# Layer normalisation without affine terms: a ring of larger tiles, normalised in place, and a last store in two parts

## The chip, the cores and the metric

The kernel runs on one core of a Trainium2 chip, alone. The metric is the device time of one execution in microseconds (us), taken as the median of several. Three engines of the core compute here: VectorE (DVE in the profile), ScalarE (ACT) and GpSimd (POOL). SyncE (SP) only issues loads. The core's 16 DMA engines move data between the chip's main memory (HBM) and the on-chip buffer of 128 partitions (SBUF). SP and ACT each have one DMA queue, which runs over all 16 engines; a DMA is cut into packets, and each engine works through its own share of them.

## The reference

```
batch, seq, dim = 32, 512, 1024        # x is float32

def reference(x, eps):
    mean = np.mean(x, axis=-1, keepdims=True)
    var = np.var(x, axis=-1, keepdims=True)
    return ((x - mean) / np.sqrt(var + eps)).astype(np.float32)
```

There are 32 x 512 = 16,384 rows of 1,024 numbers, 4 KiB each: 64 MiB are read and 64 MiB are written. Each row is normalised by its own mean and variance.

## The kernel before, in words

The rows are laid out as a matrix of 16,384 x 1,024 (L23 to L25). A tile is 4 rows on each of 128 partitions (`K = 4`, L30), 512 rows or 2 MiB, so there are 32 tiles (L33). In a tile, partition p holds 4 rows that are neighbours in HBM; a partition's part of a load or store is thus one run of 16 KiB.

For every tile the loop (L43) does this:

- L46 and L47: SP issues the load into `xt`, one of six buffers (`xin`, L35).
- L51 to L57: for each of the 4 rows DVE runs two `bn_stats` over 512 columns each (L53) and one `bn_aggr` (L57) that joins them to a mean and a variance in `mv`.
- L59, L61, L65: DVE makes `negmean`, `vpe` (variance plus eps) and its reciprocal `ivar`, for the four rows at once.
- L68: ACT takes the square root of `ivar`, which gives `rstd`.
- L71: POOL multiplies `negmean` and `rstd` to `nmr`.
- L75: ACT makes four rows of `yt` from `xt`, as `rstd * x + nmr`, one instruction a row. `yt` is one of six other buffers (`yout`, L36).
- L84: ACT issues the store of `yt`.

Six buffers of 16 KiB a partition for `xt` and six for `yt` come to 192 KiB a partition. The framework sets the order of instructions on each engine itself from the dependencies, and it puts in the waits: a load into a buffer waits until ACT has read what was there, and L75 waits until the store of the earlier content of its `yt` has landed. The framework deals eight semaphores to the DMAs in turn (the trace has eight of them, with 128 landings each, 16 for a DMA). A DMA waits until the DMA that had its semaphore before has landed.

Of the kernel before, what the change touches and what calls it, by code (L numbers as in the profile page):

```python
# [1 line left out]

# [4 lines left out]


@with_exitstack  # L10
def kernel(
    ctx: ExitStack,
    tc: tile.TileContext,
    x: bass.AP,
    eps: bass.AP,
    out: bass.AP,
):
    nc = tc.nc
    P = nc.NUM_PARTITIONS

    eps_val = float(eps) if not isinstance(eps, bass.AP) else 1e-5

    x2 = x.flatten_outer_dims()  # L23
    o2 = out.flatten_outer_dims()
    N, D = x2.shape  # L25
    BN_MAX = nc.vector.BN_STATS_FMAX
    assert D % BN_MAX == 0
    NSUB = D // BN_MAX

    K = 4  # L30
    rows_per_tile = P * K
    assert N % rows_per_tile == 0
    ntiles = N // rows_per_tile  # L33

    xin = ctx.enter_context(tc.tile_pool(name="xin", bufs=6))  # L35
    yout = ctx.enter_context(tc.tile_pool(name="yout", bufs=6))  # L36
    st = ctx.enter_context(tc.tile_pool(name="st", bufs=4))

    fdt = mybir.dt.float32
    AF = mybir.ActivationFunctionType  # L40
    ALU = mybir.AluOpType

    for t in range(ntiles):  # L43
        rows = slice(t * rows_per_tile, (t + 1) * rows_per_tile)

        xt = xin.tile([P, K, D], fdt)  # L46
        nc.sync.dma_start(out=xt, in_=x2[rows].rearrange("(p k) d -> p k d", p=P))  # L47

        stats = st.tile([P, K, NSUB, 6], fdt)
        mv = st.tile([P, K, 2], fdt)  # L50
        for k in range(K):  # L51
            for s in range(NSUB):
                nc.vector.bn_stats(  # L53
                    out=stats[:, k, s, :],
                    in_=xt[:, k, s * BN_MAX : (s + 1) * BN_MAX],
                )
            nc.vector.bn_aggr(out=mv[:, k, :], in_=stats[:, k, :, :])  # L57
        negmean = st.tile([P, K], fdt)
        nc.vector.tensor_scalar_mul(out=negmean, in0=mv[:, :, 0], scalar1=-1.0)  # L59
        vpe = st.tile([P, K], fdt)  # L60
        nc.vector.tensor_scalar(  # L61
            out=vpe, in0=mv[:, :, 1], scalar1=eps_val, scalar2=None, op0=ALU.add
        )
        ivar = st.tile([P, K], fdt)
        nc.vector.reciprocal(out=ivar, in_=vpe)  # L65

        rstd = st.tile([P, K], fdt)
        nc.scalar.activation(out=rstd, in_=ivar, func=AF.Sqrt, bias=0.0, scale=1.0)  # L68

        nmr = st.tile([P, K], fdt)  # L70
        nc.gpsimd.tensor_mul(out=nmr, in0=negmean, in1=rstd)  # L71

        yt = yout.tile([P, K, D], fdt)
        for k in range(K):
            nc.scalar.activation(  # L75
                out=yt[:, k, :],
                in_=xt[:, k, :],
                func=AF.Identity,
                bias=nmr[:, k : k + 1],
                scale=rstd[:, k : k + 1],  # L80
            )

        dst = o2[rows].rearrange("(p k) d -> p k d", p=P)
        nc.scalar.dma_start(out=dst, in_=yt)  # L84


# [1 line left out]
_INS = ['x', 'eps']  # L88
_OUTS = [((32, 512, 1024), 'float32')]
#: Inputs that are plain numbers.  # L90
_NUMBERS = {'eps': 1e-05}


# [26 lines left out]
```

## Time and profile before

| what | value |
| --- | --- |
| median of 8 runs | 321.3 us (321.08 to 321.51) |
| the profiled execution, its own time | 321.35 us |
| its span, first to last profiled instruction | 319.3 us |
| DVE busy | 181.6 us, 57% of the span |
| ACT busy | 154.2 us, 48% |
| POOL busy | 6.6 us, 2% |
| moved by DMA | 134.27 MB, mean 421 GB/s |
| one `bn_stats` of 128 x 512 (L53), mean | 664 ns, 256 of them |
| one row on ACT (L75), mean | 1,227 ns, 128 of them |
| a load, issue to landing, median | 38.4 us |
| a store, issue to landing, median | 15.5 us |

The execution's own time is 2.05 us more than the span; what lies around the span isn't in the profile. The span is what the steps of the work can be read from. The DMA row of the profile gives the mean busy share of the 16 DMA engines: 1.00 says that all sixteen were busy, 0.06 that one of sixteen was. Packets of one engine can overlap by some nanoseconds, so that a share of 1.01 can be read. Beside the answers of the views, the trace holds a record of each DMA packet (start, duration, size and queue, but not the number of the engine), and single packets are quoted from there.

### The profile page before, as it was taken

Reading aid. Unit: us, or ns where it says so; the run is one execution under the profiler, and the core shown is the slowest. Engines: PE = TensorE matmul, PEld = TensorE weight load, DVE = VectorE, ACT = ScalarE, POOL = GpSimd, SP = SyncE. Lnnn points to the kernel's source line nnn. Section 1 sums busy time; section 2 is a strip of 40 time slices with the busy share of each in tenths; the row PEclk is TensorE's granted clock in tenths of the full one; section 3 lists DMA queues with packets and bytes.
Section 4 is the critical chain, followed back from the end, with each engine's and each line's share of the span. In section 5 each row is a group of like instructions: output and inputs, shape, how many; then the busy total and the mean of one; then the engine's idle time right before and its main releaser. Section 6 shows DMA issues by size and latency. Waiting matters only on the chain.

```text
span 319.3 us, 926 instructions
## 1 busy us (share of the span) xinstructions
DVE 181.6 (57%) x480; ACT 154.2 (48%) x161; POOL 6.6 (2%) x36
## 2 busy tenths in 40 slices
DVE  0999764457754477544676535765446744467610
ACT  1147491651907419074380833808347091470970
POOL 0000000000000000000000000000000000000000
DMA  7999999999999999999999999999999999999995
GB/s 298 427 394 426 435 435 431 431 429 429 428 431 434 433 431 427 429 429 433 435 435 431 428 429 429 429 431 435 433 433 426 426 431 435 433 433 413 419 427 220
DMA packets 9222, 134.27 MB, mean 421 GB/s; under 512 B 1024, under 2 KB 1024, under 8 KB 1024
## 3 DMA queue, kind: packets, MB, share of 16 engines
q1 hardware_dynamic: 4608, 67.11, 49.6%
q10 hardware_dynamic: 4608, 67.11, 49.2%
q14 instruction: 6, 0.05, 0.0%
HBM read 67.11 MB, written 67.11 MB: 420 GB/s over the span
## 4 chain that ended last, share of the span: by engine, by line
DMA 84%; ACT 4%; issue 4%; DVE 4%; SPq 1%; POOLq 0%; POOL 0%; ACTq 0%; DVEq 0%
DMA xt<-in_x_dram 84%; ACT yt L75 4%; DVE stats L53 3%; SPq L47 1%; DVE mv L57 0%; ACT rstd L68 0%; DVE ivar L65 0%; DVE negmean L59 0%; POOLq L115 0%; POOL nmr L71 0%; DVE vpe L61 0%; ACTq L84 0%; DVEq L65 0%; DVEq L59 0%; ACTq L75 0%
## 5 line engine op out<-in xcount | busy, mean ns | idle before, releaser
L53 DVE BATCH_NORM_STATS2 stats<-xt 128x6 f32<-128x512 f32 x256 | 159.4, 664 | 115.6 <-DMA xt<-in_x_dram 115.6
L75 ACT ACTIVATE yt<-xt,nmr,rstd 128x1024 f32<-128x1024 f32 x128 | 146.7, 1227 | 4.7 <-POOL nmr L71 4.5
L68 ACT ACTIVATE rstd<-ivar 128x4 f32<-128x4 f32 x32 | 6.5, 204 | 149.9 <-DVE ivar L65 149.3
L57 DVE BATCH_NORM_AGGREGATE mv<-stats 128x2 f32<-128x12 f32 x128 | 25.1, 196 | 1.1
L71 POOL TENSOR_TENSOR nmr<-negmean,rstd 128x4 f32<-128x4 f32 x32 | 6.3, 198 | 298.1 <-ACT rstd L68 298.1
L65 DVE RECIPROCAL ivar<-vpe 128x4 f32<-128x4 f32 x32 | 5.7, 178 | 3.0
L59 DVE TENSOR_SCALAR negmean<-mv 128x4 f32<-128x4 f32 x32 | 5.4, 170 | 3.1
L61 DVE TENSOR_SCALAR vpe<-mv 128x4 f32<-128x4 f32 x32 | 5.2, 162 | 0.0
L68 ACT ACT_TABLE_LOAD x1 | 1.3, 1283 | 0.7 <-PEq L101 0.7
L101 POOL MEMSET const-float32-0.0<- 128x1 f32 x1 | 0.1, 98 | 0.2 <-issue 0.2
L101 POOL MEMSET const-uint8-127<- 128x1 uint8 x1 | 0.1, 102 | 0.0
L101 POOL MEMSET const-bfloat16-1.0<- 128x1 bf16 x1 | 0.1, 101 | 0.0
L101 POOL MEMSET const-float32-1.0<- 128x1 f32 x1 | 0.1, 98 | 0.0
## 6 DMA issues: line engine op xcount, KB each, us to landing
xt<-in_x_dram SPq DMA_DIRECT2D x32, 2048.0 KB, 38.4
out_dram<-yt ACTq DMA_DIRECT2D x32, 2048.0 KB, 15.5
```

The costliest lines, as they stand in the source:

```text
L47: nc.sync.dma_start(out=xt, in_=x2[rows].rearrange("(p k) d -> p k d", p=P))
L53: nc.vector.bn_stats(out=stats[:, k, s, :], in_=xt[:, k, s * BN_MAX : (s + 1) * BN_MAX],)
L57: nc.vector.bn_aggr(out=mv[:, k, :], in_=stats[:, k, :, :])
L59: nc.vector.tensor_scalar_mul(out=negmean, in0=mv[:, :, 0], scalar1=-1.0)
L61: nc.vector.tensor_scalar(out=vpe, in0=mv[:, :, 1], scalar1=eps_val, scalar2=None, op0=ALU.add)
L65: nc.vector.reciprocal(out=ivar, in_=vpe)
L68: nc.scalar.activation(out=rstd, in_=ivar, func=AF.Sqrt, bias=0.0, scale=1.0)
L71: nc.gpsimd.tensor_mul(out=nmr, in0=negmean, in1=rstd)
L75: nc.scalar.activation(out=yt[:, k, :], in_=xt[:, k, :], func=AF.Identity, bias=nmr[:, k : k + 1], scale=rstd[:, k : k + 1],)
L101: nc = _bacc.Bacc("TRN2", target_bir_lowering=False, num_devices=1)
```

## The change

The new kernel has one ring of 48 rows a partition (192 KiB) in the place of the two pools. Its tiles are of 8 rows, 15 of them, then one of 6 and one of 2 (`TILES`): 32 KiB, 24 KiB and 8 KiB a partition. Six tiles of 8 rows fill the ring. ACT writes the normalised rows over the loaded ones, and the store reads the ring. So a load into a place of the ring waits for the store of what was there, six tiles before.

The arithmetic runs in groups of up to 4 rows, 33 in all. ACT takes the square root of the variance plus eps (the bias of the activation), DVE takes the reciprocal of it, and one `scalar_tensor_tensor` on DVE makes `nmr`. `negmean`, `vpe` and POOL's multiplication are gone. The instructions of each engine are in the order of the program text (`manual_schedule`). `STORE` is 16, more than a tile has, so each tile has one store, after its last group. The last store, that of the tile of 2 rows, is issued as two DMAs, one of partitions 0 to 119 and one of partitions 120 to 127.

```diff
+TILES = (8, 8, 8, 8, 8, 8, 8, 8, 8, 8, 8, 8, 8, 8, 8, 6, 2)
+RING = 48
+GROUP = 4
+STORE = 16
...
-    K = 4
-    rows_per_tile = P * K
-    ntiles = N // rows_per_tile
-
-    xin = ctx.enter_context(tc.tile_pool(name="xin", bufs=6))
-    yout = ctx.enter_context(tc.tile_pool(name="yout", bufs=6))
+    ring_pool = ctx.enter_context(tc.tile_pool(name="ring", bufs=1))
...
+    ring = ring_pool.tile([P, RING, D], fdt)
+    eps_t = const.tile([P, 1], fdt)
+    def load(t):
+        K, row, pos = plan[t]
+        rows = slice(row * P, (row + K) * P)
+        nc.sync.dma_start(
+            out=ring[:, pos : pos + K, :],
+            in_=x2[rows].rearrange("(p k) d -> p k d", p=P),
+        )
...
-        negmean = st.tile([P, K], fdt)
-        nc.vector.tensor_scalar_mul(out=negmean, in0=mv[:, :, 0], scalar1=-1.0)
-        vpe = st.tile([P, K], fdt)
-        nc.vector.tensor_scalar(
-            out=vpe, in0=mv[:, :, 1], scalar1=eps_val, scalar2=None, op0=ALU.add
+        std = st.tile([P, GROUP], fdt, name="std")
+        nc.scalar.activation(
+            out=std[:, :G], in_=mv[:, :G, 1], func=AF.Sqrt, bias=eps_t, scale=1.0
         )
-        ivar = st.tile([P, K], fdt)
-        nc.vector.reciprocal(out=ivar, in_=vpe)
-        rstd = st.tile([P, K], fdt)
-        nc.scalar.activation(out=rstd, in_=ivar, func=AF.Sqrt, bias=0.0, scale=1.0)
-        nmr = st.tile([P, K], fdt)
-        nc.gpsimd.tensor_mul(out=nmr, in0=negmean, in1=rstd)
+        rstd = st.tile([P, GROUP], fdt, name="rstd")
+        nc.vector.reciprocal(out=rstd[:, :G], in_=std[:, :G])
+        nmr = st.tile([P, GROUP], fdt, name="nmr")
+        nc.vector.scalar_tensor_tensor(
+            out=nmr[:, :G],
+            in0=mv[:, :G, 0],
+            scalar=-1.0,
+            in1=rstd[:, :G],
+            op0=ALU.mult,
+            op1=ALU.mult,
+        )
...
             nc.scalar.activation(
-                out=yt[:, k, :],
+                out=xt[:, k, :],
                 in_=xt[:, k, :],
...
+    def store(t, o, n):
+        K, row, pos = plan[t]
+        rows = slice(row * P, (row + K) * P)
         dst = o2[rows].rearrange("(p k) d -> p k d", p=P)
-        nc.scalar.dma_start(out=dst, in_=yt)
+        src = ring[:, pos + o : pos + o + n, :]
+
+        cuts = ((0, 120), (120, P)) if t == len(TILES) - 1 else ((0, P),)
+        for a, b in cuts:
+            nc.scalar.dma_start(out=dst[a:b, o : o + n, :], in_=src[a:b])
+    plan = []
+    row = pos = 0
+    for K in TILES:
+        if pos + K > RING:
+            pos = 0
+        plan.append((K, row, pos))
+        row += K
+        pos += K
+    with tc.manual_schedule():
+        nc.vector.memset(eps_t, eps_val)
+        for t, (K, row, pos) in enumerate(plan):
+            load(t)
+            sent = 0
+            for g in range(0, K, GROUP):
+                G = min(GROUP, K - g)
+                group(ring[:, pos + g : pos + g + G, :], G)
+                if g + G - sent >= STORE or g + G == K:
+                    store(t, sent, g + G - sent)
+                    sent = g + G
```

More of the change, by code (lines that the diff above doesn't have):

```diff
@@ L26 @@
     BN_MAX = nc.vector.BN_STATS_FMAX
-    assert D % BN_MAX == 0
     NSUB = D // BN_MAX
-    K = 4
-    rows_per_tile = P * K
-    assert N % rows_per_tile == 0
-    ntiles = N // rows_per_tile
-    xin = ctx.enter_context(tc.tile_pool(name="xin", bufs=6))
-    yout = ctx.enter_context(tc.tile_pool(name="yout", bufs=6))
+    assert sum(TILES) * P == N
+    ring_pool = ctx.enter_context(tc.tile_pool(name="ring", bufs=1))
     st = ctx.enter_context(tc.tile_pool(name="st", bufs=4))
+    const = ctx.enter_context(tc.tile_pool(name="const", bufs=1))
     fdt = mybir.dt.float32
@@ L41, with group @@
     ALU = mybir.AluOpType
[L43 to L51, printed above, removed]
+    ring = ring_pool.tile([P, RING, D], fdt)
[7 more added lines that the diff above has]
+        )
+    def group(xt, G):
+        stats = st.tile([P, GROUP, NSUB, 6], fdt, name="stats")
+        mv = st.tile([P, GROUP, 2], fdt, name="mv")
+        for k in range(G):
             for s in range(NSUB):
@@ L57 @@
             nc.vector.bn_aggr(out=mv[:, k, :], in_=stats[:, k, :, :])
-        negmean = st.tile([P, K], fdt)
-        nc.vector.tensor_scalar_mul(out=negmean, in0=mv[:, :, 0], scalar1=-1.0)
-        vpe = st.tile([P, K], fdt)
-        nc.vector.tensor_scalar(
-            out=vpe, in0=mv[:, :, 1], scalar1=eps_val, scalar2=None, op0=ALU.add
-        )
-        ivar = st.tile([P, K], fdt)
-        nc.vector.reciprocal(out=ivar, in_=vpe)
-        rstd = st.tile([P, K], fdt)
-        nc.scalar.activation(out=rstd, in_=ivar, func=AF.Sqrt, bias=0.0, scale=1.0)
-        nmr = st.tile([P, K], fdt)
-        nc.gpsimd.tensor_mul(out=nmr, in0=negmean, in1=rstd)
-        yt = yout.tile([P, K, D], fdt)
-        for k in range(K):
+        std = st.tile([P, GROUP], fdt, name="std")
+        nc.scalar.activation(
+            out=std[:, :G], in_=mv[:, :G, 1], func=AF.Sqrt, bias=eps_t, scale=1.0
+        )
+        rstd = st.tile([P, GROUP], fdt, name="rstd")
[9 more added lines that the diff above has]
+        )
+        for k in range(G):
             nc.scalar.activation(
-                out=yt[:, k, :],
+                out=xt[:, k, :],
                 in_=xt[:, k, :],
```

## The prediction

> **What bounds the kernel now.** I read the page first: the busy row, the DMA row by slices, the queues, the chain.
>
> ```profile
> span 319.3 us, 926 instructions
> ...
> DVE 181.6 (57%) x480; ACT 154.2 (48%) x161; POOL 6.6 (2%) x36
> ...
> DMA  7999999999999999999999999999999999999995
> ...
> q1 hardware_dynamic: 4608, 67.11, 49.6%
> q10 hardware_dynamic: 4608, 67.11, 49.2%
> ...
> DMA 84%; ACT 4%; issue 4%; DVE 4%; SPq 1%; POOLq 0%; POOL 0%; ACTq 0%; DVEq 0%
> ```
>
> No compute engine passes 57%. The DMA engines are full in all slices but the first and the last, loads and stores take half of them each, and 84% of the chain is loads. So only three things can shorten the span: fewer nanoseconds a byte, the start, and the tail. For those I asked for the busy time in chosen stretches (columns: length, DVE, ACT, POOL, clock, share of the 16 DMA engines, GB/s).
>
> ```profile
> 1.75:3.00 1.25, 0.00 (x0) 0.26 (x1) 0.00 (x0) 1.00 1.12 236
> ...
> 20.00:24.00 4.00, 4.00 (x10) 0.20 (x1) 0.20 (x1) 1.00 0.98 352
> 24.00:288.00 264.00, 155.04 (x412) 133.66 (x140) 5.56 (x28) 1.00 1.01 431
> ...
> 294.00:302.00 8.00, 4.01 (x12) 6.97 (x7) 0.20 (x1) 1.00 0.92 391
> 302.00:315.00 13.00, 2.17 (x8) 7.24 (x8) 0.20 (x1) 1.00 1.02 435
> 315.00:316.00 1.00, 0.00 (x0) 0.00 (x0) 0.00 (x0) 1.00 0.28 115
> 316.00:318.00 2.00, 0.00 (x0) 0.00 (x0) 0.00 (x0) 1.00 0.06 25
> ```
>
> For 264 us the rate is flat at 431 GB/s. From 294 to 302 the engines lack work for a moment (0.92 against 1.01). The last row matters most: 0.06 is 1/16, **one engine working alone for 2 us** after the others are done.
>
> The packet records say why. Fifteen engines end between 315.5 and 316.0, most near 315.6; one ends at 318.14, with four 16 KiB packets more to do. In the steady stretch (after 26 us) only six packets last over 660 ns, where the others take about 611; each follows an 8 KiB packet of queue 14, kind "instruction", that is code fetched for an engine, of 309 ns. Four of them chain to the late engine (29.5, 101.5, 180.2, 249.1 us; the next packet then takes 1,144 to 1,232 ns), so it loses 0.31 + 0.57, or 0.88 us, each time, 3.5 us in all. The two others (82.4 and 239.8 us; the next packet takes 849 and 856 ns) lie on another engine and cost 0.55 us each. Part of the late engine's lag doesn't show at the end, since the others starved at 294 to 302 and it didn't.
>
> **The change, part by part**, against the profiled execution: last packet 318.14, span 319.3 (1.16 later), own time 321.35 (2.05 more). The median, 321.3, is within 0.05 of that.
>
> *Larger packets.* Each engine moves 8 partitions of every tile: 288 records a queue and engine are 32 x 8 packets and 32 marks of 4 bytes that tell of completion. A 16 KiB packet starts 607 ns after the one before it, an 8 KiB one occupies 305 ns; 2 x 305 - 607 leaves about 3 ns a packet that don't scale. Before, an engine has 512 data packets; after, 2 x (15 x 8 + 8 + 8) = 272. That is 240 x 3 ns = 0.72 us less. Rounding of the records allows 1 to 5 ns (0.2 to 1.2 us), and nothing is gained if the hardware cuts 32 KiB in two. I take 0.72. Marks fall from 64 to 35 an engine at 5 ns: 0.15 us. Together **0.87 us** on all engines.
>
> *The last store in two.* 120 of 128 partitions are 15 engines' shares of 8; the natural reading is that one engine gets nothing. It is spared 8 packets of 8 KiB, 8 x 305 ns = **2.44 us**. The 8 remaining partitions go to up to eight others, one packet of 0.31 us each. If the spared engine is the late one, it ends at 318.14 - 0.87 - 2.44 = **314.83**.
>
> *The starved stretch.* From 294 to 302 the share is 0.09 under 1.01, 0.7 us of 8. The timeline shows the cause: ACT's queue holds a finished store behind the square root of the next tile (`yt` done at 285.0, store issued at 294.80, just after `rstd` at 294.74). In the new order the store follows its own rows at once. The stretch should close, 0.7 us for the fifteen. They then end at 315.6 - 0.87 - 0.7 + 0.31 = **314.3**, ahead of the late engine.
>
> *Does the ring starve the engines?* First store: a tile of 4 MiB lands near 13.5 us (two tiles of 2 MiB do, by the load's landings). DVE needs 5.0 us for four rows (eight `bn_stats` at 0.575, four `bn_aggr` at 0.11) and about 0.9 for square root, reciprocal, `nmr` and the hand-overs, as the rows from 38.9 to 40.0 have it; two groups and ACT's last 4.6 give 30 us, against 19.6 before. Until then loads have the engines alone, so they are some 12 MiB ahead, and with both queues served alike that stays so: when the last load lands, 12 MiB or 29 us of stores remain. The last tile needs about 14 us for its arithmetic and that of the tile ahead of it. So the tail is covered; without cover a late last tile would cost up to those 14 us. Load t+6 waits for store t and, if the eight semaphores go round in the order of issue, load t+4 waits for load t to land. Behind that wait SP has only later loads. When store 0 lands, near 50 us, loads 0 to 3 have landed (12 MiB at full rate by 30 us, 4 at half rate since), and two whole loads, 39 us at half rate, are still queued. So the wait costs nothing; uncovered, a load's wait would cost as much as it lasts.
>
> *Arithmetic.* DVE loses 96 small operations of 162 to 178 ns, gains 66 such and a wait on ACT's square root in each group: 33 x 5.9 = 195 us, under the DMA's 313. ACT's 4.6 us for four rows fit into DVE's 5.0, so the square root is not held. POOL drops out. All this is hidden by the DMA; uncovered it would be about 0.4 us a group.
>
> *Start.* First packet at 1.77, slow first packets (0.72 us an engine over 611 ns each) and the dip at 20 to 24, with 0.65 us: none is touched. I cost them at nothing; bound by the dip's own size both ways.
>
> *Code fetches.* DVE goes from 480 to 451 profiled instructions; four fetches may become three, 0.9 us less lag. What a fetch costs beside 32 KiB packets isn't shown: the packet after it lost 0.57 us, as little as that again or, if the loss grows with the packet, twice. I keep 0.57.
>
> Sum: the late engine decides, 314.83 + 1.16 = 315.99 of span, + 2.05 = **318.0 us**. With three fetches the fifteen decide at 314.3: 317.5.
>
> [...]
>
> [...]
>
> **Rivals.**
>
> *The spared engine isn't the late one.* Speaking for it: the records have no engine numbers. Against: an engine with a fixed extra duty all run long is more likely at an end of the numbering, and a cut at 120 leaves out an end. That is judgement, and the largest risk. The late engine saves 0.87 and gains 0.31: 317.58, span 318.74, **320.8**; a cut that spares nobody gives the same less 0.3.
>
> *The last store runs slowly.* A store of 120 partitions isn't in the trace. From below nothing; from above the first packets of the run, about twice 611 ns: 2.44 us more on the fifteen, 316.7, **320.0** at most.
>
> *A fetch costs more beside larger packets.* Twice the loss, 4 x 0.57 = 2.3 us on the late engine: **320.3**.
>
> *Slower: 32 KiB packets move fewer bytes a nanosecond.* The place is the steady stretch; with 240 such packets an engine, each nanosecond more costs 0.24 us. It turns slower than before (3.9 us more, 321.9) when a packet occupies over 1,211 + 16 ns. At 2% more, 24 ns, it is 5.8 us: **323.8**. For it: after a fetch, a single packet of 1,144 to 1,232 ns shows that packets normally hide something of about 0.6 us, which a larger one might hide worse. Against: from 8 to 16 KiB the time only doubles.
>
> *It doesn't do what it says* (32 KiB cut in two): 0.7 us, 318.7, inside the first case.
>
> **How the numbers follow.** First case 0.66, its own range 317.1 to 319.0. Wrong engine 0.13, slow last store 0.08, dearer fetch 0.08, slower packets 0.05. The range runs from three fetches with the larger packet gain (317.1) to the wrong engine (320.8); above it is half of that case and the slower one, below it little. A measurement of this kernel tells about 0.2% from no change, 0.64 us, so faster means under 320.66: 0.66 + 0.08 + 0.05 of the dearer fetch + 0.05 of the wrong engine = 0.84. Within: 0.11. Slower: 0.05.
>
> **What would show it.** Larger packets: data packets near 1,211 ns, 431 GB/s rising to about 432. Spared engine: no stretch of share 0.06 over 2 us before the end. Stores in order: no dip to 0.92 near the end. Fetches: four packets of queue 14 on one engine and what the packet after each loses. Wrong would be a DMA share under 0.99 between 30 and 310 us, a lone engine at the end, or packets over 1,227 ns.

## The result, and the profile after

The changed kernel takes **324.22 us** (median of 11 runs, 321.82 to 327.10). The kernel before, run beside it, takes 321.19 us (31 runs). The ratio is 1.0075 (95% interval 1.0059 to 1.0092): slower, where I forecast 318.0 us. Executions over 1.5% longer than the fastest of the same kernel are left out of this and all later ratios (two here, five of twelve in the most scattered kernel below), but not out of the medians, so that a ratio can lie below the quotient of the medians.

The profiled execution took 324.22 us itself, 1.82 more than its span. These are lines of its page: span, busy times, DMA row, queues, and the shares of the chain.

```profile
span 322.4 us, 736 instructions
...
DVE 187.8 (58%) x451; ACT 159.4 (49%) x162; POOL 0.2 (0%) x4
...
DMA  8999999999999999999999999999999999999993
...
q1 hardware_dynamic: 2448, 67.11, 49.6%
q10 hardware_dynamic: 2455, 67.11, 48.4%
...
DVE 45%; another core or an unknown queue 25%; DMA 15%; ACT 6%; issue 1%; SPq 0%; ACTq 0%
```

The packets are nearly halved, as planned, and the engines are as full as before. The chain now names DVE where it named the DMA. That doesn't make DVE the bound: its busy time is 58% of the span. The chain goes back by who released whom, and each tile's store waits for its arithmetic while the DMA engines work through a long queue. The busy time in chosen stretches says where the time is (columns as in the prediction).

```profile
24.00:288.00 264.00, 167.87 (x402) 143.17 (x146) 0.00 (x0) 1.00 1.00 427
...
294.00:302.00 8.00, 4.01 (x12) 5.32 (x7) 0.00 (x0) 1.00 1.02 441
302.00:315.00 13.00, 0.09 (x1) 2.37 (x2) 0.00 (x0) 1.00 0.97 411
315.00:316.00 1.00, 0.00 (x0) 0.00 (x0) 0.00 (x0) 1.00 0.72 270
316.00:318.00 2.00, 0.00 (x0) 0.00 (x0) 0.00 (x0) 1.00 0.45 156
318.00:320.00 2.00, 0.00 (x0) 0.00 (x0) 0.00 (x0) 1.00 0.17 70
320.00:322.40 2.40, 0.00 (x0) 0.00 (x0) 0.00 (x0) 1.00 0.02 10
```

Three things differ from the kernel before. The stretch from 294 to 302 is full (1.02, it was 0.92). The long stretch moves 427 GB/s in place of 431 **at the same busy share**: engines that are busy but move less have packets that last longer. And the end is no longer fifteen engines together and one late: the share falls in steps over 7 us.

The packet records explain the second point. A 32 KiB packet normally occupies 1,213 ns, and 1,209 ns after its start the next one begins. But about every 20 us, near the moment when a store of stores 0 to 9 is complete, some 9 to 29 packets, most of them of loads, last 50 to 930 ns longer. I call the time of packets beyond the usual one for their size (611 ns for 16 KiB, 1,213 for 32, 912 for 24, 309 for 8) their **excess**. It was 1.93 us an engine before and is 5.32 now, 3.39 more. In both kernels about 1.5 us of it comes in the first 40 us; 0.48 of the new one comes after 300 us, in the last two stores. The long packets aren't shared out evenly, so the engines drift apart: the first engine ends its part of the load of tile 13 at 242.4 us, the last at 248.5.

For the end, I followed each engine's packets back from its last one (a packet begins where the one before it ends). One engine has no packet of the last store and ends at 313.62. The engine that ends last, at 321.13, carries 8 packets of the 120-partition store and then one of the 8-partition store. Followed back, it is the engine that had the code fetches (38.3, 117.3, 204.2 and 292.6 us). Its packets of the last store take 309 ns but for one of 328; one of its 24 KiB packets, of the store before, took 1,922 ns in place of 912. So **the cut spared another engine and gave the late one a packet more**.

One guess of mine can be read in the waits of SP's queue (us in total, times, longest):

```profile
SPq L52 <- DMA out_dram<-ring: 215.3, 10, 41.9
SPq L151 <- DMA out_dram<-ring: 88.0, 2, 67.2
```

The loads wait for stores, as the ring demands. Six loads were issued by 3.6 us; I had thought the fifth might wait for the first. The semaphores hold up a store instead: store 10 waited from 207.7 to 230.0 us until load 12 had landed. The share is 0.99 there, since loads keep the engines busy.

### The profile page after: what moved, and what is told of

Its sections match the earlier page's. It is cut to its first block, busy times and chain, and to the rows that moved or that the text cites. A ratio compares the mean times of both kernels' runs of the same rounds, so it can differ in the third digit from the quotient of the medians.

```text
span 322.4 us, 736 instructions
## 1 busy us (share of the span) xinstructions
DVE 187.8 (58%) x451; ACT 159.4 (49%) x162; POOL 0.2 (0%) x4
## 3 DMA queue, kind: packets, MB, share of 16 engines
q1 hardware_dynamic: 2448, 67.11, 49.6%
## 4 chain that ended last, share of the span: by engine, by line
DVE 45%; another core or an unknown queue 25%; DMA 15%; ACT 6%; issue 1%; SPq 0%; ACTq 0%
DVE stats L62 36%; DMA ring<-in_x_dram 15%; DVE mv L66 6%; ACT ring L83 4%; ACT std L68 3%; DVE rstd L72 2%; DVE nmr L74 1%; SPq L52 0%; ACTq L99 0%
## 5 line engine op out<-in xcount | busy, mean ns | idle before, releaser
L62 DVE BATCH_NORM_STATS2 stats<-ring 128x6 f32<-128x512 f32 x256 | 159.3, 664 | 79.9 <-DMA ring<-in_x_dram 79.9
L83 ACT ACTIVATE ring<-ring,nmr,rstd 128x1024 f32<-128x1024 f32 x128 | 148.4, 1229 | 14.6 <-DVE nmr L74 14.6
L68 ACT ACTIVATE std<-mv,eps_t 128x4 f32<-128x4 f32 (+1 forms) x33 | 9.8, 297 | 129.8 <-DVE mv L66 107.1
L66 DVE BATCH_NORM_AGGREGATE mv<-stats 128x2 f32<-128x12 f32 x128 | 26.7, 209 | 4.4
L72 DVE RECIPROCAL rstd<-std 128x4 f32<-128x4 f32 (+1 forms) x33 | 5.8, 177 | 28.0 <-ACT std L68 28.0
L74 DVE SCALAR_TENSOR_TENSOR nmr<-mv,rstd 128x4 f32<-128x4 f32 (+1 forms) x33 | 5.4, 162 | 1.1
```

The source lines that it names most:

```text
L62: nc.vector.bn_stats(out=stats[:, k, s, :], in_=xt[:, k, s * BN_MAX : (s + 1) * BN_MAX],)
L68: nc.scalar.activation(out=std[:, :G], in_=mv[:, :G, 1], func=AF.Sqrt, bias=eps_t, scale=1.0)
L72: nc.vector.reciprocal(out=rstd[:, :G], in_=std[:, :G])
L74: nc.vector.scalar_tensor_tensor(out=nmr[:, :G], in0=mv[:, :G, 0], scalar=-1.0, in1=rstd[:, :G], op0=ALU.mult, op1=ALU.mult,)
L83: nc.scalar.activation(out=xt[:, k, :], in_=xt[:, k, :], func=AF.Identity, bias=nmr[:, k : k + 1], scale=rstd[:, k : k + 1],)
```

## The experiments

The theory after the result had two parts. First, the cut costs time in itself and spares the wrong engine. Second, the long load packets come with 32 KiB packets (theory 'packets' in what follows), or with the ring, or with both. The rival to the first was that the cut helps and only the long packets hide it; to the second, that a 32 KiB packet is simply slower.

### The cut

**The last store whole.** In the changed kernel:

```diff
-        cuts = ((0, 120), (120, P)) if t == len(TILES) - 1 else ((0, P),)
+        cuts = ((0, P),)
```

> The changed kernel with its last store issued as one DMA. [...] Rival 'cut' (the last store in two parts, with packets of 8 KiB drawn out to 0.6 us while other engines end their part, is what costs): 2 us or more faster, 322 or under.

Measured 322.93 us (320.01 to 324.93, 12 runs), ratio 1.0038 [1.0011, 1.0064]. That lies between the two forecasts: within 1 us of 324.2 if the engine that ends last only loses its one extra packet of 0.31 us, 322 or under if the cut is what costs. The medians say that the cut costs 1.3 us here, little more than the scatter lets one tell (the intervals of the two ratios overlap a little), and the packets of the whole store have no excess. Without the cut the kernel is still above the whole range of the prediction, so the cut alone isn't the miss. The excess before it stays (3.9 us an engine in all), and so does a spread of 5 us between executions of one and the same kernel.

**Which engine is late.** The last store as eight DMAs of 100, 7, 6, 5, 4, 3, 2 and 1 partitions, so that the count of small packets tells the engines apart:

```diff
+        cuts = ((0, P),)
+        if t == len(TILES) - 1:
+            e = (0, 100, 107, 113, 118, 122, 125, 127, P)
+            cuts = tuple(zip(e, e[1:]))
```

> Asks for the number of the engine that lags, not for a time. The last store goes out as eight DMAs of 100, 7, 6, 5, 4, 3, 2 and 1 partitions. [...]

One run, 324.1 us. Six engines have no packet of this store and end near 311. The engine of the four fetches at 38.6, 117.4, 203.3 and 290.8 us has ten packets and then four single ones and ends at 320.93; another has six single ones and ends last, at 321.17. So the counts tell these two engines apart; the number that the run asked for stays unknown, since the records hold none. This execution has no bursts of long load packets (after 36 us at most four at a time, 1.95 us an engine in all loads, the first 36 us included), though its kernel differs from the changed one in the last store alone.

**The cut alone, in the kernel before** (4 rows a partition, 16 KiB packets):

```diff
-        nc.scalar.dma_start(out=dst, in_=yt)
+        cuts = ((0, 120), (120, P)) if t == ntiles - 1 else ((0, P),)
+        for a, b in cuts:
+            nc.scalar.dma_start(out=dst[a:b], in_=yt[a:b])
```

> The kernel before with its last store (4 rows, 16 KiB packets) issued as two DMAs of 120 and 8 partitions, and nothing else. Theory 'cut' (packets of the DMA of 120 partitions take up to twice their time, and the spared engine isn't the late one): each of fifteen engines has 0.6 us more, and up to 4.9 us if every packet doubles; 323 to 326. Rival (the packets keep 611 ns): 321.7 to 322.2 if the late engine gets one packet more, 318.7 if it is the spared one.

Measured 325.70 us (325.39 to 326.23, 4 runs), ratio 1.0138 [1.0121, 1.0155]: 4.4 us slower by the cut alone. These are the stretches of its end:

```profile
302.00:315.00 13.00, 2.66 (x10) 7.73 (x8) 0.20 (x1) 1.00 1.02 364
315.00:316.00 1.00, 0.00 (x0) 0.00 (x0) 0.00 (x0) 1.00 0.22 66
316.00:318.00 2.00, 0.00 (x0) 0.00 (x0) 0.00 (x0) 1.00 1.06 287
318.00:320.00 2.00, 0.00 (x0) 0.00 (x0) 0.00 (x0) 1.00 0.75 188
```

Between 316 and 318 the engines that have work are busy and move 287 GB/s; at such a share they moved 435 before. (A row counts each packet in full in the stretch where it begins, which matters in so short a one: by the packet records, cut at the edges, the share is 0.89, that is 14 engines, and they move 253 GB/s.) Half of the store's 16 KiB packets last some 590 ns or more longer than 611, that is about twice as long; one in four keeps its time within 70 ns, and the longest lasts 1,771. Twice the time is the bound that the prediction took for a slow last store from the first packets of the run; what draws the packets out isn't shown. The spared engine ends at 311.15, one other at 316.6, the remaining fourteen at 319.7 to 322.35.

**The cut with 16 KiB packets in the ring, and without it.** The first kernel changes `TILES` alone; the second, run later, has the last store whole as well:

```diff
-TILES = (8, 8, 8, 8, 8, 8, 8, 8, 8, 8, 8, 8, 8, 8, 8, 6, 2)
+TILES = (4,) * 31 + (2, 2)
```

> The changed kernel with tiles of 4 rows (31 of them, then 2 and 2): ring, arithmetic and cut of the last store stay, packets are 16 KiB. Theory 'packets': load packets are 611 ns throughout but for the first store, the excess over nominal falls from 5.3 to about 2 us an engine, and the time is 318.5 to 320.5. Rival 'ring' (a load that waits for a store ties the beginnings of loads and stores together, whatever the size): the long load packets stay, 322 to 325.

> The ring of tiles of 4 rows (16 KiB packets) with its last store whole. Theory: the cut cost that kernel the drawn-out packets of its last store, 1.75 us an engine, and one packet of 0.31; what else it loses is the stretch of share 0.76 from 300 to 310 us, which stays. So 321.5 to 322.8 against 324.4. Rival (the end is set by the starved stretch alone, the cut lies beside it): 324 to 324.5.

With the cut 324.37 us (324.35 to 324.78, 4 runs), ratio 1.0103 [1.009, 1.0116]; whole 321.84 us (321.73 to 322.07, 10 runs), 1.0021 [1.0012, 1.003]. The cut costs 2.5 us; that is most of why the first kernel misses the 318.5 to 320.5 us of theory 'packets', though whole it is still above them. The same two microseconds of the end, with the cut and then without:

```profile
316.00:318.00 2.00, 0.00 (x0) 0.00 (x0) 0.00 (x0) 1.00 1.05 225
```

```profile
316.00:318.00 2.00, 0.00 (x0) 0.00 (x0) 0.00 (x0) 1.00 1.07 442
```

Equal busy share in the rows, half the bytes. The steady stretch has no long packets in either but for single ones and a few near 85 us, and it is tight, 430 GB/s. What this ring loses it loses near the end, at shares of 0.79 to 0.88 between 294 and 312, as ACT's queue waits for semaphores that late loads hold (with the cut, ACT's square root waited five times for a load that it doesn't read, 99.4 us in all, 33.7 at most; whole, 99.5 us).

### The long load packets

**32 KiB packets without a ring.** The kernel before with 8 rows a tile and three buffers in each pool:

```diff
-    K = 4
+    K = 8
...
-    xin = ctx.enter_context(tc.tile_pool(name="xin", bufs=6))
-    yout = ctx.enter_context(tc.tile_pool(name="yout", bufs=6))
+    xin = ctx.enter_context(tc.tile_pool(name="xin", bufs=3))
+    yout = ctx.enter_context(tc.tile_pool(name="yout", bufs=3))
```

> The kernel before with tiles of 8 rows and three buffers in each pool in the place of six: 32 KiB packets, but no ring and not in place. Theory 'packets': long load packets at the hand-over of stores as in the changed kernel, 322.5 to 326, with a spread of several us between executions. Rival 'ring': no long packets after the first store, 320 to 321.5 unless the three buffers leave the engines idle, which the DMA share would show.

Measured 324.59 us (324.47 to 324.72, 4 runs), ratio 1.0107 [1.0094, 1.0121]. Its stretches:

```profile
40.00:288.00 248.00, 134.15 (x340) 122.82 (x119) 2.62 (x13) 1.00 1.00 432
294.00:302.00 8.00, 6.60 (x19) 0.81 (x2) 0.20 (x1) 1.00 0.54 230
```

No long packets and 432 GB/s: a 32 KiB packet isn't slower by itself. The time is lost to starvation (0.54), three buffers being too few.

**16 KiB packets in the order of the changed kernel.** Each load and store as two DMAs of 4 rows, in the changed kernel with its cut; then only the stores, and only the loads, with the last store whole:

```diff
+        src = x2[rows].rearrange("(p k) d -> p k d", p=P)
+        for o in range(0, K, 4):
+            n = min(4, K - o)
+            nc.sync.dma_start(
+                out=ring[:, pos + o : pos + o + n, :], in_=src[:, o : o + n, :]
+            )
...
+            for h in range(0, n, 4):
+                m = min(4, n - h)
+                nc.scalar.dma_start(
+                    out=dst[a:b, o + h : o + h + m, :], in_=src[a:b, h : h + m, :]
+                )
```

> The changed kernel with each load and store of 8 rows issued as two DMAs of 4 rows: same tiles, same ring and order of the arithmetic, packets of 16 KiB. Theory 'packets': no long load packets, 318.5 to 320.5. Rival 'tile' (it is the size of the tile, the late first store or the bursts of the arithmetic, not the packet): as the changed kernel, 322.5 to 326.

> The changed kernel with the last store whole and every store as two DMAs of 4 rows, so that stores have 16 KiB packets and loads 32 KiB. If large store packets lengthen the load packets beside them: no long load packets in the steady stretch, excess near 2 us an engine, 320 to 321.5. If large load packets are what is drawn out: the excess stays at 3.5 to 5.5 us, 322 to 324.5.

> The same the other way round: loads as two DMAs of 4 rows with 16 KiB packets, stores in 32 KiB, last store whole. If large store packets lengthen the loads: the excess stays, 322 to 324.5. If large load packets are what is drawn out: it goes to about 2 us an engine, 320 to 321.5. If it goes in both this and the run with 16 KiB stores, only the pair of sizes does it.

Both in 16 KiB: 323.70 us (323.56 to 323.77, 4 runs), 1.0079 [1.0066, 1.0092], no long load packets, 430 GB/s, and a drawn-out last store (1.65 us an engine). Stores alone: 328.13 us (327.21 to 328.94, 4 runs), 1.0211 [1.0187, 1.0234]; loads alone: 323.68 us (322.99 to 324.2, 4 runs), 1.0072 [1.0055, 1.0088]. In both halves long packets remain (3.9 and 4.7 us an engine in all), of loads and of stores alike, so neither queue's size alone ends them. With loads alone in 16 KiB it is the 16 KiB load packets that are long: 2.1 us an engine after 40 us, where the stores' 32 KiB packets have 0.7. Which of the two sizes matters isn't told. The kernel with the stores alone in 16 KiB lies outside both forecasts, 5 us above the one with the whole store, which has the same excess (3.9). The packet records show how: fifteen engines end between 314.5 and 319.3 us, and one ends alone at 324.2.

**A smaller ring**, the last store whole:

```diff
-RING = 48
+RING = 32
```

> The changed kernel with its last store whole and a ring of 4 tiles in the place of 6. Theory 'depth' (the long load packets come with more than 3 loads of 32 KiB packets waiting in the queue; the kernel with three buffers a pool had none): no long load packets in the steady stretch, little spread, 319.5 to 321.5 unless the engines starve. Theory 'coupling' (they come with loads that are issued when a store lands, so that both start at one moment): they stay or grow, 322 to 326, spread of 2 us and more.

> The same with a ring of 5 tiles. Theory 'depth': between the rings of 4 and of 6, at most half of the excess of 6. Theory 'coupling': as the ring of 6, 321 to 325.

With four tiles 320.20 us (319.96 to 321.44, 6 runs), ratio **0.9975** [0.9962, 0.9988], faster than the kernel before. With five (`RING = 40`) 321.95 us (320.04 to 325.67, 10 runs), 1.0019 [0.9989, 1.0048], as scattered as with six. The ring of four:

```profile
24.00:288.00 264.00, 165.36 (x397) 141.35 (x145) 0.00 (x0) 1.00 1.00 430
...
315.00:316.00 1.00, 0.00 (x0) 0.00 (x0) 0.00 (x0) 1.00 0.06 25
316.00:318.00 2.00, 0.00 (x0) 0.00 (x0) 0.00 (x0) 1.00 0.05 20
```

The end has its old form again: fourteen engines done between 314.0 and 314.9, one at 315.25, one (0.06, 0.05) alone until 317.56, the one of the four fetches. After the first 40 us a burst of long packets shows once, at 66 to 69 us; the excess is 2.4 us in all. From this I took the number of queued 32 KiB loads for the cause. Three runs tried that.

**Three tiles** (`RING = 24`):

> A ring of 24 rows, three tiles of 8 rows, the last store whole. If fewer queued loads are only better, 319.8 to 320.4 us. But with three tiles a load waits for the store of three tiles before, and a tile needs about 20 us to load at the shared rate, some 12 to 14 for its arithmetic and some 20 to store: 3 x 20 us of cycle leaves little over. If the DMA engines starve, a share under 0.97 shows in the steady stretch and the time is 324 us or more. I hold starving likelier, 6 in 10.

Measured 332.9 us (331.95 to 334.36, 5 runs), 1.0365 [1.0343, 1.0387].

```profile
24.00:288.00 264.00, 153.62 (x369) 133.17 (x136) 0.00 (x0) 1.00 0.98 411
...
302.00:318.00 16.00, 9.55 (x24) 9.69 (x11) 0.00 (x0) 1.00 0.91 390
```

The time is that of the starving case, but the share, 0.98, says that starvation is the smaller part: the excess is 9.5 us an engine, the most of all runs, and more than half of it comes where loads run with few stores or none (from 84 to 93 us 2.65 MB of load packets begin and 0.52 MB of store packets, from 144 to 150 us 2.13 MB and none). Fewer loads in the queue gave more long packets.

**Loads held back to four in the ring of 48 rows**, by a DMA of 4 bytes ahead of each load that waits for the store four tiles before:

```diff
+            if t >= HOLD:
+                old = plan[t - HOLD][2]
+                nc.sync.dma_start(
+                    out=ring[0:1, old : old + 1, 0:1],
+                    in_=x2[0:1, 0:1].rearrange("(p k) d -> p k d", p=1),
+                )
             load(t)
```

> The changed kernel with its last store whole and its ring of 48 rows, but each load from the fifth on stands behind a DMA of 4 bytes that waits for the store of the tile four before it. So only four tiles are under way at once, as in a ring of 32 rows, while the loads still go round in 48 rows. If the number of queued 32 KiB loads makes the load packets long, this gives what the ring of 32 rows gave, 320.2 us (319.9 to 321.0), with no stretch of long load packets after 80 us and under 2.5 us of excess an engine. If it is the place in the buffer (192 KiB a partition gone round in), it gives what the whole last store gave in the ring of 48, about 322.9 (321.8 to 324), with 3.5 us of excess or more.

Measured 325.02 us, from 320.36 to 333.15 in 12 runs, 1.0039 [1.0012, 1.0066]. The profiled execution is the longest one (333.15), and much of it isn't long packets but a starved stretch:

```profile
280.00:294.00 14.00, 6.03 (x15) 2.96 (x5) 0.00 (x0) 1.00 1.01 418
294.00:302.00 8.00, 5.71 (x14) 6.57 (x7) 0.00 (x0) 1.00 0.38 159
```

Long packets remain in both queues (5.05 us an engine). Neither forecast holds. The added DMAs spoil the test: they are 13 more waits, and 26 more packets in the loads' queue (2,474, where it had 2,448).

**The same without added DMAs**: four places that move through all 48 rows, in the ring of 32 rows with the store whole:

```diff
-RING = 32
+RING = 48
...
-    for K in TILES:
-        if pos + K > RING:
-            pos = 0
+    for t, K in enumerate(TILES):
+        if t % 4 == 0 and t < 16:
+            pos = (16, 11, 5, 0)[t // 4]
```

> The ring of 32 rows with the last store whole gave 320.20 us, that of 48 rows 322.93. Here the four places begin at rows 16, 11, 5 and 0 in the four rounds, so that each load still waits for the store four tiles before, with no DMA added, and all 48 rows are used in the course of the run. If the number of tiles under way is what counts, 320.2 us (319.9 to 321.0) and no stretch of long load packets after 80 us. If it is the place in the buffer, 321.5 us or more with over 3 us of excess an engine. After the last two runs I hold neither likelier.

Measured 320.04 us (319.98 to 321.03, 6 runs), 0.9968 [0.9956, 0.998], no burst of long packets after 69.1 us. So the place in the buffer doesn't matter (320.20 us in 32 rows), and with this arithmetic a ring that keeps four tiles under way stays clear of them.

**The cut in the ring of 32 rows**, the changed kernel with `RING = 32` alone:

> The changed kernel with a ring of 32 rows and its last store still in two DMAs. Whole, the last store gave 320.20 us in this ring. The cut alone cost 2.5 us in a ring of 16 KiB packets and 4.4 us in the kernel before, where the engines are in step, and 1.3 us in the changed kernel, where they are not. If the drawn-out packets of the 120 partitions are the cost, and they need engines that are in step, this gives 320.2 + 1.2 to 320.2 + 2.5, that is 321.4 to 322.7. By my prediction's step, that the cut frees the late engine, it would be under 319.5.

Measured 321.20 us (320.33 to 321.7, 11 runs), 0.9998 [0.999, 1.0007]: 1.0 us for the cut, a little under what I expected. The excess after 300 us is 1.16 us an engine, but the engine that ends last, at 318.17, has none of it: its eight packets of the store begin near 315.4 us, while the other engines are ending theirs (314.8 to 316.8), and take 309 ns each. What the cut adds on that engine is a ninth packet of 0.31 us; what else makes up the 1.0 us isn't told.

### The code fetches

**Fewer instructions on DVE, in the kernel before.** `negmean`, `vpe` and `rstd` go to GpSimd, `ivar` and ACT's square root go away:

```diff
-        nc.vector.tensor_scalar(
+        nc.gpsimd.tensor_scalar(
             out=vpe, in0=mv[:, :, 1], scalar1=eps_val, scalar2=None, op0=ALU.add
         )
-        ivar = st.tile([P, K], fdt)
-        nc.vector.reciprocal(out=ivar, in_=vpe)
...
-        nc.scalar.activation(out=rstd, in_=ivar, func=AF.Sqrt, bias=0.0, scale=1.0)
+        nc.gpsimd.tensor_tensor(out=rstd, in0=vpe, in1=mhalf, op=ALU.pow)
+        negmean = st.tile([P, K], fdt)
+        nc.gpsimd.tensor_scalar_mul(out=negmean, in0=mv[:, :, 0], scalar1=-1.0)
```

> The kernel before with negmean, vpe and rstd (as a power of -0.5, in the place of reciprocal and square root) on GpSimd: 12 instructions a tile on VectorE in the place of 15, 384 in all. Theory 'fetches' (one engine is late by 0.88 us for each 8 KiB of VectorE's code): three fetches in the place of four on the late engine, which ends 0.9 us earlier; 320.2 to 320.7. Rival (the late engine is late for another reason, or GpSimd's longer chain delays the stores): 321 or more.

Measured 320.26 us (319.92 to 320.68, 9 runs), ratio 0.9972 [0.9962, 0.9981], within the forecast. Its busy row, the stretch that starved before, and the end:

```profile
DVE 168.2 (53%) x384; ACT 149.9 (47%) x129; POOL 53.4 (17%) x133
```

```profile
294.00:302.00 8.00, 5.27 (x12) 4.35 (x4) 0.35 (x2) 1.00 1.00 428
...
315.00:316.00 1.00, 0.00 (x0) 0.00 (x0) 0.00 (x0) 1.00 0.12 49
316.00:318.00 2.00, 0.00 (x0) 0.00 (x0) 0.00 (x0) 1.00 0.02 8
```

DVE has 96 instructions fewer, and the late engine's fetches are three (37.8, 134.7, 232.9 us). It ends at 316.99, 1.14 us earlier than before. The others end earlier too, most near 314.5 in place of 315.6, and the stretch that starved is full (1.00, it was 0.92), which fits the prediction's reading of it: there is no square root on ACT now that could hold a store. So the distance to the others doesn't show the fetch; the late engine's own packets do. After 26 us it is never idle in either kernel, and its fetches and the excess of its other packets come to 3.55 us before and 2.62 here, 0.93 less. That is one fetch and the packet after it. The remaining 0.2 us lie in the first 26 us.

**Both gains**: the ring of 32 rows, the last store whole, the small arithmetic on GpSimd; then the same with 48 rows.

```diff
+        vpe = st.tile([P, GROUP], fdt, name="vpe")
+        nc.gpsimd.tensor_scalar(
+            out=vpe[:, :G], in0=mv[:, :G, 1], scalar1=eps_val, scalar2=None, op0=ALU.add
+        )
+        rstd = st.tile([P, GROUP], fdt, name="rstd")
+        nc.gpsimd.tensor_tensor(
+            out=rstd[:, :G], in0=vpe[:, :G], in1=mhalf[:, :G], op=ALU.pow
+        )
...
+        nc.gpsimd.tensor_mul(out=nmr[:, :G], in0=negmean[:, :G], in1=rstd[:, :G])
```

> The ring of 32 rows with the last store whole, and the small arithmetic of a group on GpSimd as in the run that took it from VectorE: VectorE is left with 384 instructions. That took away one code fetch of four and gave 0.9 us there. In the ring of 32 rows the late engine ended at 317.6 us and the others at 314.0 to 314.9, so one fetch less gives 320.2 - 0.9 = 319.3 (319.0 to 319.7), if the fetches decide the end there too. If they don't, 320.2 as without it. Slower than 320.8 if the longer chain of a group (VectorE, GpSimd, ScalarE) lets the four tiles of the ring run dry.

> The fastest kernel (ring of 32 rows, last store whole, small arithmetic on GpSimd, 319.01 us with five times within 0.05 us) with a ring of 48 rows and nothing else changed. If the ring of six tiles itself brings long load packets and uneven engines, as with the changed kernel's own arithmetic (322.93 against 320.20 us, 2.7 more), this gives 321 to 323 us with a spread of 2 us or more between its times. If the long packets had to do with the changed kernel's arithmetic or its hand-overs, 319.0 to 319.5.

With 32 rows **319.01 us** (318.96 to 319.01, 5 runs), ratio 0.9933 [0.9921, 0.9944]: the fastest kernel found, 2.2 us under the kernel before, and five executions within 0.05 us.

```profile
24.00:288.00 264.00, 154.02 (x338) 134.18 (x117) 49.37 (x116) 1.00 1.00 432
...
315.00:316.00 1.00, 0.00 (x0) 0.00 (x0) 0.00 (x0) 1.00 0.04 16
316.00:318.00 2.00, 0.00 (x0) 0.00 (x0) 0.00 (x0) 1.00 0.00 0
```

With 48 rows 319.73 us (319.04 to 319.95, 5 runs), 0.9953 [0.994, 0.9965]. I expected 321 to 323 if the ring of six itself brings the long packets; it has no burst after 34.5 us, only four single long packets besides those that follow a fetch. **So that theory falls too**: six 32 KiB loads under way are not enough to cause them.

**What stays open.** Bursts of long load packets came with 32 KiB packets in at least one queue and the changed kernel's arithmetic, in rings of 48 rows, and again in that of 24 rows; in the ring of 40 rows only the scatter of the times speaks for them, since the profiled execution has at most three at a time after 37.6 us. They didn't come with 16 KiB in both queues, in two pools, with four tiles of this arithmetic (but for one burst near 66 us, and where extra DMAs were added), or with six tiles and the small arithmetic on GpSimd. They differ from one execution to another: the same kernel with the whole store ran from 320.01 to 324.93 us. One profile stands for each kernel, so a kernel whose profile has no burst may still have them in other executions. Neither the size, nor the number of loads, nor the place explains this alone. I don't know the mechanism.

## Why the prediction was wrong

*What bounds the kernel*: right. Every kernel here runs its long stretch at a DMA share of 0.98 to 1.01.

*Larger packets*, 0.87 us: the mechanism is right, and the size is at the upper end that I gave for rounding (2 x 607 - 1,209 is 5 ns a packet, 1.2 us for 240). And the rate is 432 GB/s in kernels without bursts (8 rows in two pools, fastest kernel), against 431.

*The last store in two*, 2.44 us less: **this is the step that failed**, in both its halves, each of which I had as a rival. The spared engine isn't the late one (by 2.44 us, and one more packet of 0.31), and the DMA of 120 partitions runs at up to twice its time a packet (560 to 680 ns in place of 309, about 1,200 in place of 611). The cut never gained anything: it costs 1.0, 1.3, 2.5 and 4.4 us in the four kernels that were run with and without it. It costs most, 4.4, where the store has 16 KiB packets; of the three with 8 KiB packets it costs most, 2.5, in the ring of 16 KiB tiles, where without the cut all engines end within 0.2 us of each other, and 1.0 and 1.3 where the last engine comes to the store after the others and runs its own packets at 309 to 328 ns. That this is what sets the cost is my reading; no run changes it alone. My chance of 0.13 for the wrong engine rested on the judgement that an engine with extra duties lies at an end of the numbering. Nothing in the trace said so.

*The starved stretch*, 0.7 us: right, 1.02 in place of 0.92 at 294 to 302.

*The ring doesn't starve the engines*: right for 48 rows, with a wrong guess on the semaphores that cost nothing there. In the ring of 16 KiB tiles the held stores did cost time, near the end (shares of 0.79 to 0.88).

*Arithmetic hidden, start untouched*: right. DVE's 167.87 us lie under 264 us of full DMA.

*Code fetches*: the cost is right, 0.31 for the fetch (one of the four took 0.72) and some 0.53 for the packet after it, so the dearer fetch is refuted. Four stayed four at 451 instructions; at 384 there are three.

*Slower packets*: this rival's 323.8 is nearest to what was measured, but for a reason that isn't its own. It asked for more than 1,227 ns a packet in general, and the usual packet takes 1,213. What happened has no term in my sum: bursts of long packets, most of them of loads, 2.9 us an engine (3.39 less the 0.48 at the end). The trace before had shown one such burst, and I read it as a thing of the start that the change doesn't touch: in the dip at 20 to 24 us the engines are busy (0.98) and move 352 GB/s, and 47 load packets between 20.7 and 25.9 us last 56 to 713 ns longer, 0.70 us an engine. In the changed kernel bursts come about every 20 us. Whether they are the same thing isn't shown, and why they come stays open.

The late engine's sum with the measured terms: 314.83 forecast, + 2.44 not spared, + 0.31 for the second part's packet, + 3.39 of excess is 320.97; the trace has 321.13. That it comes so near is partly luck: 3.39 is a mean over the engines, and the late engine has more than its share (7.0 us of excess after 30 us, where the mean is 4.6), while the larger packets, at 5 ns each, gave more than the 0.87 in the sum. Without the cut and without the long packets the kernel is my "wrong engine" case less that packet, 320.5 by the prediction, and the ring of 32 rows measured 320.20. By the medians the miss of 6.2 us is 3.7 for the cut (2.44 forecast as gain, 1.3 lost) and 2.7 for the bursts (322.93 us in the ring of 48 rows with the whole store, 320.20 in that of 32), 6.4 together; the scatter of the medians is larger than what is left over.

The range failed because it took one rival at a time: two of them held together, and the third loss, the bursts, was one that the trace before had shown only once, at the start.

## What to carry to other kernels

Before work is moved off a late DMA engine, find out which one it is: packets of counted small DMAs told the engines apart in one run (the one of the fetches had ten and then four single ones). Here it was cheaper to remove what makes it late: with 384 instructions on DVE in place of 480 there were three fetches in place of four, which gave 0.9 us where the cut lost up to 4.4. When a ring is made deeper or its packets larger, look at the busy share and the GB/s of the same stretch together, and at the spread between executions: a share of 1.00 at fewer GB/s (427 here, 431 before) is lost time that no wait shows.

## What the runs showed of the hardware that I had not expected

- A store of 120 of 128 partitions drew at least half of its 16 KiB packets out from 611 to about 1,200 ns in the kernel before, and its 8 KiB packets from 309 to some 560 to 680 ns on some engines of the changed kernel.
- One 8 KiB code fetch on the DMA engine that ends last delayed the whole kernel before by about 0.9 us: one fetch less, 0.93 us less on that engine, and 320.26 us in place of 321.21.
- Load packets of 32 KiB (and of 16 KiB beside stores of 32 KiB) lasted up to about twice as long (1,213 ns and up to 930 more in the changed kernel) in bursts of 3 to 6 us, all over the 16 engines, in some kernels and some executions; at worst 9.5 us an engine of excess, in the ring of 24 rows, where stores were long too.
- A store of the changed kernel waited 22 us for the semaphore of a load that has nothing to do with it, and with loads queued the DMA share stayed at 0.99.
